# A recurrence of 32 heads: chunk by chunk over all heads, instead of four groups of heads inside the products

## The chip, the cores and the metric

The kernel runs on one core of a Trainium2 chip. The metric is the device time of one execution in microseconds, lower is better. Five engines matter: PE (TensorE, matrix products), ACT (ScalarE), DVE (VectorE), POOL (GpSimd) and SP (SyncE, which here issues every DMA). PEld stands for PE's weight loads, which overlap its matmuls.

## The reference, cut to what matters

The model has two layers; the change is in the first one's mixer (RWKV-7, 32 heads of 64, 272 tokens: 16 meta tokens and 256 others).

```python
r, k, v = xr @ w_rkv[0], xk @ w_rkv[1], xv @ w_rkv[2]
g = sigmoid(xg @ g1) @ g2
kk = normalized(k * k_k);  k = k * (1 + (a - 1) * k_a)
def step(S, inp):                       # per head, S is 64 x 64
    sa = einsum('bhvk,bhk->bhv', S, a_t)            # a_t = -kk
    S = S * w_t + sa[..., None] * b_t + v_t[..., None] * k_t    # b_t = kk * a
    return S, einsum('bhvk,bhk->bhv', S, r_t)
y = lax.scan(step, S0, ...)
y = group_norm(y) * ln_w + ln_b
bonus = sum(r * k * r_k, per head) * v
out = ((y + bonus) * g) @ w_o
```

Both layers have an MLP of width 8192 behind the mixer; the second mixer is gated linear attention. All of it is float32 in and out.

## The kernel before, in words

Activations lie transposed: 16 tiles (`KT`) of 128 features by `T` = 272 tokens. A large product splits each weight tile of 128x1024 into a high part (L134, ACT) and the rest (L135, DVE), and does three matmuls of 272 columns for each 128x128 block (`mm3`, L140 to L142).

The mixer works in this order. First come the r-products, the low-rank terms and gates' inner part. Then the **k-products** (L452 on): for each f of 16 feature tiles (two heads each) a product `proj`, a chain on ACT and DVE that makes the scaled keys and queries `bk` and `ar` (four `put`s, each a product over four chunks of 64 tokens and one over the last 16), their stores to DRAM (`bkd`, `ard`), a head sum `ss` (L465) and the bonus head sum `rk` (L480) on PE. Into these the first group's scores and its inversion are woven.

The recurrence is done in chunks: four of 64 tokens and a short one of 16. For a chunk, `scores` (L416) multiplies `BK` by `AR` for all token pairs, masked by DVE into `AM`; `invert` turns the triangular blocks of 32 rows into their inverses on DVE (30 steps of two operations, L268 `upd` and `sysA`, between transposes L431 to L449), and `merge` (L535, L545) joins two blocks of 32 to one of 64 on PE. Then follow, for a chunk: `centre` (values, L558), `inner` (L579), `state` (L598, L601), `solve` (L611), `carry` (L620) and `learn` (L626) for the new state, `emit` (L636) for the output, `keys` (L569) as transposes for learn. A chunk must wait for the state of the one before.

Heads go in **four groups of eight** (`NG` = 4), one group through its five chunks after the other. PE's order is written out by hand (`manual_schedule`): `R(n)` puts n steps of three product matmuls between the recurrence's batches, as the table `GAPS` says, 448 such steps in all: the v-products (`v_proj`, 16 x 16 steps), then the output products in pieces (`outA` over the first half of the heads, `outB` over the rest) as groups finish. While group g runs, group g + 1 gets its scores, inversion and merge; `norm` of group g - 1 makes the group norm and its gate product (L665).

PE, ACT, DVE and SP each take their instructions in order; PE's order is by hand here, the others' by a planner.

Of the kernel before, what the change touches and what calls it, by code (L numbers as in the profile page):

```python
# [23 lines left out]
TP = 288  # L24
# [19 lines left out]


GAPS = [[(4, 3), (4, 3), (8, 7), (8, 7), (6, 6)],
# [3 lines left out]

MARK = [134, 214, 286]


class Kern:
# [17 lines left out]
    def t(self, pool, shape, tag, bufs=1, dt=F32):  # L72
        return pool.tile(shape, dt, tag=tag, bufs=bufs, name=self.nm(tag))

# [49 lines left out]
    def wload(self, src, prio=2000):  # L124
        nc = self.nc
        with self.tc.high_priority(offset=prio) if prio else ExitStack():
            raw = self.t(self.wp, [P, 1024], "raw", self.raw_bufs)
            nc.sync.dma_start(raw, src)
            hi = self.t(self.wp, [P, 1024], "hi", self.hi_bufs, F32R)
            lo = self.t(self.wp, [P, 1024], "lo", self.hi_bufs, F32R)  # L130
            n = 1024 // self.split_parts
# [134 lines left out]
    def rwkv(self, done):  # L266
# [7 lines left out]
        bkd, ard = (self.t(self.dp, [KT, P, 576], n) for n in ("bkd", "ard"))  # L274
# [26 lines left out]
        rstd = self.rstd_from(ep, ss, T, 1.0 / D, NORM_EPS, "kn", 2)  # L301
# [35 lines left out]
        xr = [self.t(self.xp, [P, 2, T], "x", KT, F32R) for _ in range(KT)]  # L337
# [49 lines left out]
        st2 = [[self.t(ep, [P, 576], n, 2) for i in range(2)] for n in ("bk", "ar")]  # L387
        for x in st2[0] + st2[1]:
            nc.gpsimd.memset(x[:, 512:], 0.0)
        Wf = self.t(ep, [P, T + 1], "W")  # L390
        nc.gpsimd.memset(Wf[:, 0:1], 1.0)
        W = Wf[:, 1:]

        def put(dst, slot, a, b, skip=0):
            v = dst[:, :512].rearrange("q (c s t) -> q c s t", c=4, s=2)[:, :, slot]
            tt(v, a[:, : 4 * C].rearrange("q (c t) -> q c t", c=4), b[:, : 4 * C].rearrange("q (c t) -> q c t", c=4))
            o = 512 + 32 * slot
            tt(dst[:, o + skip : o + 16], a[:, 4 * C + skip :], b[:, 4 * C + skip :])

        def fetch(g, dst, src, a=0, b=576):  # L400
            nc.sync.dma_start(dst[g % 2][:, :, a:b], src[4 * g : 4 * g + 4, :, a:b].rearrange("f p n -> p f n"))

        def load(g):
            fetch(g, BKs, bkd)
            fetch(g, ARs, ard)

        def scores(g, c):
            BK, AR, AM, AMr = (b[g % 2] for b in (BKs, ARs, AMs, AMrs))
            n = C if c < NC4 else 32
            cs = slice(c * 128, c * 128 + 2 * n)  # L410

            pv = [self.ptr().rearrange("p (h m) -> p h m", h=4)[: 2 * n, :, : 2 * n] for _ in range(2)]
            for p in range(4):
                for q in range(2):
                    rows = slice(64 * q, 64 * q + 64)
                    nc.tensor.matmul(pv[q][:, p], BK[rows, p, cs], AR[rows, p, cs], start=True, stop=True)  # L416
            dst, mk = (AM[:, c], self.maskA) if c < NC4 else (AMr, self.maskR)
            for q in range(2):
                tt(dst[:, q::2], pv[q], mk.unsqueeze(1).to_broadcast([2 * n, 4, 2 * n]))

        def invert(g):
            AM, AMr = AMs[g % 2], AMrs[g % 2]
            X = sysA
            diag = lambda u: AM[64 + 32 * u : 96 + 32 * u, :, :, 32 * u : 32 * u + 32].rearrange("p c h t -> p t c h")
            part = [slice(8 * k, 8 * k + 8) for k in range(4)]
            nc.gpsimd.memset(X[64:96], 0.0)
            for u in range(2):
                for k in part:  # L430
                    nc.vector.transpose(X[32 * u : 32 * u + 32, k], diag(u)[:, k])  # L431
                    yield
            for k in part[:2]:
                nc.vector.transpose(X[96:128, k], AMr[32:64, :, k].rearrange("p h t -> p t h").unsqueeze(2)
                                    .to_broadcast([32, 8, 4, 8]))
                yield
            nc.gpsimd.memset(X.rearrange("p a b -> p (a b)")[:, ::33], 1.0)
            for s in range(1, 31):
                n, m = 31 - s, s
                w = self.t(lp, [P, 256], "upd", 1)[:, : n * m].rearrange("p (a b) -> p a b", a=n)  # L440
                tt(w, X[:, s + 1 :, s : s + 1].to_broadcast([P, n, m]), X[:, s : s + 1, :m].to_broadcast([P, n, m]))
                tt(X[:, s + 1 :, :m], X[:, s + 1 :, :m], w, ALU.add)
                yield
            for k in part:
                nc.vector.transpose(t11.rearrange("p c h s -> p s c h")[:, k], X[0:32].rearrange("p t s -> p s t")[:, k])
                yield
            for u in range(2):
                for k in part:
                    nc.vector.transpose(diag(u)[:, k], X[32 * u : 32 * u + 32, k])  # L449
                    yield  # L450

        for f in range(KT):  # L452
            r = rr[f]
            bk, ar = st2[0][f % 2], st2[1][f % 2]
# [3 lines left out]
            iW, kk, sq, kn = (self.t(ep, [P, T], n, 2) for n in ("iW", "kk", "sq", "kn"))  # L458
            nc.scalar.activation(W, ca[:, 0], AF.Exp, scale=-DECAY)
            nc.scalar.activation(iW, ca[:, 0], AF.Exp, scale=DECAY)  # L460
            nc.scalar.mul(kk, ps, self.vec("k_k", f))
            nc.scalar.activation(sq, kk, AF.Square)
# [6 lines left out]
            nc.vector.scalar_tensor_tensor(out=kk, in0=sq, scalar=1e12, in1=kk, op0=ALU.min, op1=ALU.mult)  # L469
# [6 lines left out]
            nc.vector.scalar_tensor_tensor(out=kn, in0=r, scalar=self.vec("r_k", f), in1=kn, op0=ALU.mult, op1=ALU.mult)  # L476
            put(ar, 1, r, W)
            nc.sync.dma_start(ard[f], ar)
# [3 lines left out]
            nc.vector.tensor_copy(WC[:, f], W[:, C - 1 : 4 * C : C])  # L482
            if f == 3:
                xv = mix(3, self.xp)
                early2.close()
                wl = ExitStack()
                lp = wl.enter_context(tc.tile_pool(name="wl", bufs=1, reuse_waits="tile"))
                BKs, ARs = ([self.t(lp, [P, 4, 576], n)] for n in ("BK0", "AR0"))
                AMs, AMrs = [self.t(lp, [P, NC4, 8, 128], "AM0")], [self.t(lp, [64, 8, 64], "AMr0")]
                sysA = self.t(lp, [P, 32, 32], "sysA")  # L490
                t11 = sysA.rearrange("p a b -> p (a b)")[64:96].rearrange("p (c h s) -> p c h s", c=NC4, h=8)
                nc.gpsimd.memset(sysA, 0.0)
            if f == 4:
                load(0)
            if f == 6:
                for c in range(5):
                    scores(0, c)
                inv = invert(0)
# [613 lines left out]
```

## Time and profile before

| | us |
|---|---|
| three runs: median (lowest to highest) | 2619.78 (2614.41 to 2630.18) |
| the profiled execution | 2614.87 |
| its span, first to last instruction | 2612.6 |
| PE, DVE, ACT busy | 2545.5, 1679.5, 1267.8 |
| mean granted clock of PE | 0.986 |

The profile shows one execution. Busy time of PE counts a matmul from its start to a modelled end; matmuls overlap, so a stretch with 100% busy can still hold less work than another. The granted clock is 1.0 or 0.5 at any moment; a stretch's number is the mean.

### The profile page before, as it was taken

Reading aid. Unit: us, or ns where it says so; the run is one execution under the profiler, and the core shown is the slowest. Engines: PE = TensorE matmul, PEld = TensorE weight load, DVE = VectorE, ACT = ScalarE, POOL = GpSimd, SP = SyncE. Lnnn points to the kernel's source line nnn. Section 1 sums busy time; section 2 is a strip of 40 time slices with the busy share of each in tenths; the row PEclk is TensorE's granted clock in tenths of the full one; section 3 lists DMA queues with packets and bytes.
Section 4 is the critical chain, followed back from the end, with each engine's and each line's share of the span. In section 5 each row is a group of like instructions: output and inputs, shape, how many; then the busy total and the mean of one; then the engine's idle time right before and its main releaser. Section 6 shows DMA issues by size and latency. Waiting matters only on the chain.

```text
span 2612.6 us, 47351 instructions
## 1 busy us (share of the span) xinstructions
PE 2545.5 (97%) x19308; PEld 2360.1 (90%) x19308; DVE 1679.5 (64%) x2802; ACT 1267.8 (49%) x2068; POOL 11.5 (0%) x32
## 2 busy tenths in 40 slices
PE   7998999989999999999999999999999999999998
PEld 7887988879999999999999999998888888888887
DVE  8677967764755545545546677777666656656665
ACT  5464645544544434434434455545555435445344
POOL 0000000000000000000000000000000000000000
PEclk9998999988999999999999999999999999999999
DMA  5566742323455555555555544454555555555554
GB/s 193 175 217 213 242 161 97 104 88 99 164 175 177 178 175 174 176 177 178 176 174 176 186 156 156 154 173 158 186 187 190 187 187 189 189 186 190 188 187 160
DMA packets 137193, 450.59 MB, mean 172 GB/s; under 512 B 15760, under 2 KB 23696, under 8 KB 136976
## 3 DMA queue, kind: packets, MB, share of 16 engines
q1 hardware_dynamic: 136976, 447.58, 51.0%
q8 instruction: 151, 2.47, 0.4%
q14 instruction: 66, 0.54, 0.1%
HBM read 431.53 MB, written 15.99 MB: 171 GB/s over the span
## 4 chain that ended last, share of the span: by engine, by line
PE 80%; DVE 3%; ACT 1%; issue 0%; DMA 0%; DVEq 0%; SPq 0%
PE pj L168 24%; PE pj L140 13%; PE pj L142 13%; PE pj L141 13%; PE pj L169 12%; DVE lo L135 1%; PE pt L665 0%; PE pu L950 0%; ACT hi L134 0%; PE pt L416 0%; PE pt L936 0%; DVE upd L268 0%; DVE sysA L431 0%; DVE sysA L268 0%; PE pu L601 0%
## 5 line engine op out<-in xcount | busy, mean ns | idle before, releaser
L134 ACT CAST hi<-raw 128x1024 fp32r<-128x1024 f32 (+1 forms) x834 | 813.5, 983 | 1065.9 <-PE pj L141 551.9
L135 DVE TENSOR_TENSOR lo<-raw,hi 128x1024 fp32r<-128x1024 f32 (+1 forms) x834 | 946.7, 1142 | 580.6 <-ACT hi L134 571.8
L140 PE MATMUL pj<-x,hi 128*128 128x272 f32 x2224 | 661.1, 297 | 7.4 <-ACT x L308 4.3
L142 PE MATMUL pj<-x,lo 128*128 128x272 f32 x2224 | 648.5, 292 | 0.1
L141 PE MATMUL pj<-x,hi 128*128 128x272 f32 x2224 | 646.4, 291 | 0.5 <-DVE x L268 0.5
L168 PE MATMUL pj<-x,hi 128*128 128x512 f32 x1664 | 586.1, 395 | 2.1 <-DVE cj L178 1.1
L169 PE MATMUL pj<-x,lo 128*128 128x256 f32 x1664 | 466.7, 281 | 0.8 <-DVE lo L135 0.8
L140 PEld LDWEIGHTS pj<-x,hi 128*128 128x128 f32 x2224 | 424.3, 191 | 15.2 <-ACT x L308 5.1
L141 PEld LDWEIGHTS pj<-x,hi 128*128 128x128 f32 x2224 | 426.9, 192 | 2.9 <-DVE x L268 0.7
L142 PEld LDWEIGHTS pj<-x,lo 128*128 128x128 f32 x2224 | 423.8, 191 | 1.9 <-DVE lo L135 0.7
L168 PEld LDWEIGHTS pj<-x,hi 128*128 128x128 f32 x1664 | 312.4, 188 | 76.1 <-issue 1.9
L168 PE MATMUL pj<-h,hi 128*128 128x512 f32 x1024 | 358.5, 394 | 0.0
L169 PEld LDWEIGHTS pj<-x,lo 128*128 128x128 f32 x1664 | 313.3, 188 | 1.7 <-DVE lo L135 1.1
L140 PE MATMUL pj<-h,hi 128*128 128x272 f32 x1024 | 294.7, 288 | 0.0
L142 PE MATMUL pj<-h,lo 128*128 128x272 f32 x1024 | 293.9, 287 | 0.0
L141 PE MATMUL pj<-h,hi 128*128 128x272 f32 x1024 | 293.6, 287 | 0.0
L169 PE MATMUL pj<-h,lo 128*128 128x256 f32 x1024 | 288.5, 282 | 0.0
L168 PEld LDWEIGHTS pj<-h,hi 128*128 128x128 f32 x1024 | 192.4, 188 | 44.5
L141 PEld LDWEIGHTS pj<-h,hi 128*128 128x128 f32 x1024 | 193.7, 189 | 0.0
L169 PEld LDWEIGHTS pj<-h,lo 128*128 128x128 f32 x1024 | 193.5, 189 | 0.0
L140 PEld LDWEIGHTS pj<-h,hi 128*128 128x128 f32 x1024 | 192.6, 188 | 0.0
L142 PEld LDWEIGHTS pj<-h,lo 128*128 128x128 f32 x1024 | 192.1, 188 | 0.0
(253 smaller groups left out, 2217.9 us busy)
## 6 DMA issues: line engine op xcount, KB each, us to landing
raw<-mlp_w_d SPq DMA_DIRECT2D x512, 512.0 KB, 3.3
raw<-gla_in_d SPq DMA_DIRECT2D x98, 512.0 KB, 3.3
raw<-w_rkv_d SPq DMA_DIRECT2D x80, 512.0 KB, 3.6
raw<-gla_o_d SPq DMA_DIRECT2D x32, 512.0 KB, 4.3
raw<-w_r_d SPq DMA_DIRECT2D x16, 512.0 KB, 3.3
raw<-rw_oA_d SPq DMA_DIRECT2D x16, 512.0 KB, 3.3
raw<-rw_oB_d SPq DMA_DIRECT2D x16, 512.0 KB, 3.3
ard<-ar SPq DMA_DIRECT2D x16, 288.0 KB, 3.6
```

Of the source, the lines that this page charges most:

```text
L134: nc.scalar.copy(hi[:, h], raw[:, h])
L135: nc.vector.tensor_tensor(out=lo[:, h], in0=raw[:, h], in1=hi[:, h].bitcast(F32), op=ALU.subtract)
L140: nc.tensor.matmul(out, hi[:, ws], xh, start=first, stop=False)
L141: nc.tensor.matmul(out, hi[:, ws], xl, start=False, stop=False)
L142: nc.tensor.matmul(out, lo[:, ws], xh, start=False, stop=last)
L168: nc.tensor.matmul(wide, hi[:, ws], x[kt][:, :, off : off + SEQ], start=kt == 0, stop=False)
L169: nc.tensor.matmul(ps[:, :SEQ], lo[:, ws], x[kt][:, 0, off : off + SEQ], start=False, stop=kt == nk - 1)
```

## The change: what it does

- **k-products.** All of `rk`, the scores and the inversion leave this stage. `bk` and `ar` become tiles of five chunks of 64 (the last padded with zeros), and the two products by `iW` become one of 640 elements. Stores go to `bkd` and `ard` laid out by chunk. Two small copies move from DVE to ACT.
- **v-products.** They hold all scores: 20 units of (chunk, eight heads), two per f for the first four f, then one; each unit has 16 matmuls of a 64x64 quarter instead of 8 of 64x128. `rk` is in each f. From f = 4 on, 0.34 inversion steps (`PACE`) go with each product step. An inversion now handles two chunks of all 32 heads on 128 rows; there are two, and a short one of 16 rows for the last chunk. The first inversion's merge is in here.
- **The recurrence** runs after the v-products with no product between: chunk by chunk, two halves (z = 0, 1) of 16 heads that alternate. `inner` of the next chunk is interleaved with `solve`; the state is updated by DVE in place of `carry` and four ACT operations; copies out of PSUM are shared between ACT and DVE. The second merge and all 16 gate products come behind chunk 1.
- **Norms and output products.** Seven output tiles are summed in seven banks while the 16 norms come in one after the other; the remaining nine follow as plain products.
- Operand tiles `x` of one pool become pairs (`xs`).

```diff
-GAPS = [[(4, 3), (4, 3), (8, 7), (8, 7), (6, 6)],
...
         for f in range(KT):
...
-            put(ar, 0, kk, Wf[:, :T], 1)
-            nc.vector.tensor_copy(ar[:, 0:513:128], kk[:, ::C])
-            tt(kk, kk, ca[:, 1])
-            put(bk, 1, kk, iW)
-            put(bk, 0, kn, iW)
-            nc.sync.dma_start(bkd[f], bk)
+            tt(ar[:, :, 0], five(kk), five(Wf))
+            nc.scalar.copy(ar[:, :, 0, 0], kk[:, ::C])
+            tt(kx[:, 1, :T], kk[:, :T], ca[:, 1])
+            tt(bk.rearrange("p c s t -> p s c t"), kx.rearrange("p s (c t) -> p s c t", c=5),
+               five(iW).unsqueeze(1).to_broadcast([P, 2, 5, C]))
+            nc.sync.dma_start(bkd[:, :, f].rearrange("c p n -> p c n"), bk.rearrange("p c s t -> p c (s t)"))
...
-            rk = self.pu()[:, :T]
-            nc.tensor.matmul(rk, self.bones, kn, start=True, stop=True)
-            nc.scalar.copy(r, rk)
...
-            if f > 7:
-                for _ in range(7):
-                    next(inv, None)
...
+        def uload(c, g):
+            t = slot("ring", 1024).rearrange("p (a f n) -> p a f n", a=2, f=4)
+            for i, d in enumerate((bkd, ard)):
+                nc.sync.dma_start(t[:, i], d[c][:, 4 * g : 4 * g + 4])
+            return t
+
+        def scores(t, c, g, bank):
...
+                    for u in range(2):
+                        nc.tensor.matmul(pv[q][n * u : n * u + n, p], t[rows, 0, p, C * u : C * u + n], ar,
+                                         start=True, stop=True)
...
+        def eliminate(X, n, rows):
+            for s in range(1, n - 1):
...
+                tt(w, x[:, s + 1 : n, s : s + 1].to_broadcast([k, a, m]), x[:, s : s + 1, :m].to_broadcast([k, a, m]))
+                tt(x[:, s + 1 : n, :m], x[:, s + 1 : n, :m], w, ALU.add)
+                yield
...
+        def merge1(i, banks):
+            for a in range(2):
+                am, t11, qs, pq = AMs[2 * i + a], (X, T2)[a], (TA, X)[a], banks[a]()
+                for h in range(32):
+                    o, k = 32 * (h % 4), 32 * (h // 4)
+                    nc.tensor.matmul(pq[o : o + 32, k : k + 32], am[64:96, h, 32:64], t11[64:96, h], start=True, stop=True)
+                for j in range(4):
+                    nc.scalar.copy(qs[96:128, j::4], pq[32 * j : 32 * j + 32, :256].rearrange("p (h t) -> p h t", h=8))
...
+        def sides(z, c):
+            full, n, nr, am, lo, up, at = geom(c)
+            ra, uv = ras[z, c], uvs[z, c]
+            nc.scalar.mul(uv[up, 0::2], ra[at[0]], -1.0)
+            nc.vector.tensor_scalar(out=uv[up, 1::2], in0=ra[at[1]], scalar1=-1.0, scalar2=None, op0=ALU.mult)
...
+        def solve(z, c):
...
+            for p in range(8):
+                for i in (2 * p, 2 * p + 1):
+                    o = n * (1 - i % 2)
+                    nc.tensor.matmul(pu[o : o + nu, p], am[up, 16 * z + i, :nu], uv[up, i], start=True, stop=True)
+                for i in (2 * p, 2 * p + 1) if both else ():
+                    inner1(z, c + 1, i)
+            nc.scalar.copy(uv[n : n + nu, 0::2], pu[n : n + nu])
+            nc.vector.tensor_copy(uv[n : n + nu, 1::2], pu[0:nu])
...
+        def gate(f):
+            g2 = self.t(kp, [P, 2, P], "g2", 2)
+            nc.sync.dma_start(g2, ap["g2"][f])
+            pg = self.ptr()[:, :T]
             for i in range(2):
+                nc.tensor.matmul(pg, g2[:, i], gs[i], start=i == 0, stop=i == 1)
+            nc.scalar.copy(gw(f), pg)
...
+        def norm(f):
+            sq = self.t(kp, [P, T], "ysq", 3)
+            nc.scalar.activation(sq, hres[:, f], AF.Square)
+            va = self.pm()[:, :T]
+            nc.tensor.matmul(va, self.bones, sq, start=True, stop=True)
...
         with tc.manual_schedule(engines={mybir.EngineType.PE}):
+            due = 0.0
+            for f in range(KT):
+                step = 0
+                for _ in v_proj(f):
+                    step += 1
+                    if f < 4 and step == 7 or step == 12:
+                        unit()
+                    if step == 13:
+                        rk = (self.pry if f % 2 else self.pm)()[:, :T]
+                        nc.tensor.matmul(rk, self.bones, rr[f], start=True, stop=True)
+                    if f >= 4 and merged[0] in (0, 3):
+                        due += PACE
+                        while due >= 1:
+                            due -= 1
+                            if next(inv, None) == "merge":
...
+            for c in range(5):
+                last = c == NC4
+                if c:
+                    state(0, c)
+                    learn(1, c - 1)
+                    emit(1, c - 1)
...
+                solve(0, c)
+                if c:
+                    state(1, c)
+                    if c < NC4:
+                        keys(1, c)
+                else:
+                    inner(1, 0)
+                    sides(1, 0)
+                some(inv, 4)
+                if not last:
+                    learn(0, c)
+                emit(0, c)
+                some(inv, 2)
+                solve(1, c)
+                if c < 3:
+                    bload(1, c + 1)
+                    keys(0, c + 1)
...
                 if c == 1:
                     some(inv, 99)
+                    merge1(1, (self.ptr, self.ptr))
+                    for f in range(8):
+                        gate(f)
+                    merge2(1, (self.ptr, self.ptr))
+                    for f in range(8, KT):
+                        gate(f)
...
+            norm(0)
+            norm(1)
+            NB = 7
+            pss = [b()[:, :T] for b in (self.pj, self.pj, self.ptr, self.ptr, self.pu, self.pu, self.pry)]
+            for kt in range(KT):
+                if kt + 2 < KT:
+                    norm(kt + 2)
+                ahead()
+                hi, lo = weights.pop(0)
+                for f in range(NB):
+                    self.mm3(pss[f], hi, lo, slice(f * P, f * P + P), yo[kt][:, 0], yo[kt][:, 1], kt == 0, kt == KT - 1)
```

More of the change, by code (lines that the diff above doesn't have):

```diff
@@ L400, in fetch @@
[L400 to L419, printed above, removed]
@@ L423, in invert @@
[L423 to L450, printed above, removed]
@@ new lines, in learn, with emit @@
+        def learn(z, c):
+            uv, pS = uvs[z, c], half(self.pu())
+            for i in range(16):
+                k = slice(64 * (i % 2), 64 * (i % 2) + 64)
+                nc.tensor.matmul(pS[k, i // 2], bkts[z][:, i // 2, k], uv[:, i], start=i < 2, stop=i > 13)
+            s, w = sb[:, 8 * z : 8 * z + 8], WC[:, 8 * z : 8 * z + 8, c].unsqueeze(2).to_broadcast([P, 8, HEAD])
+            if c:
+                tt(s, pS, s, ALU.add)
+            tt(s, s if c else pS, w)
+        def emit(z, c):
+            full, n, nr, am, lo, up, at = geom(c)
+            uv, ry = uvs[z, c], rys[z, c] if c else half((self.pry if z else self.pm)())
+            for i in range(16):
+                k = slice(64 * (i % 2), 64 * (i % 2) + 64)
+                nc.tensor.matmul(ry[k, i // 2, :nr], uv[: 2 * n, i], am[: 2 * n, 16 * z + i, n : n + nr],
+                                 start=c == 0 and i < 2, stop=i > 13)
+            nc.scalar.copy(hres[:, 8 * z : 8 * z + 8, c * C : c * C + nr], ry[:, :, :nr])
@@ L731, in rwkv @@
+        srcs = [s for f in range(KT) for s in pair(wv, f)] + [ap["rw_oK"][k] for k in range(KT)]
         weights = []
@@ L758, in some, with more, unit @@
                 next(it, None)
-        nothing = iter(())
+        order = [(c, g) for g in range(4) for c in range(2)] + [(c, g) for c in (2, 3) for g in range(4)]
+        order += [(4, g) for g in range(4)]
+        loaded = []
         self.split_parts = 2
-        load(1)
+        def more():
+            if order:
+                loaded.append((uload(*order[0]), *order.pop(0)))
+        def unit():
+            scores(*loaded.pop(0), self.pu if len(order) % 2 else self.ptr)
+            more()
@@ new lines, in rwkv @@
+            if merged[0] == 0:
+                while next(inv) != "merge":
+                    pass
+            bload(0, 0)
+            bload(1, 0)
+            centre(0, 0, ("x", "x"))
+            if merged[0] < 2:
+                merge1(0, (self.ptr, self.ptr))
+            keys(0, 0)
+            centre(1, 0, ("x", "x"))
+            if merged[0] < 3:
+                merge2(0, (self.ptr, self.ptr))
+            keys(1, 0)
+            inner(0, 0)
+            sides(0, 0)
+            aload(0, 1)
@@ L834, in rwkv @@
+        rec.close()
         self.split_parts = 1
+        for f in range(KT):
+            ps = pss[f] if f < NB else self.proj(pair(ap["rw_o"], f), yo, T)
+            tt(hres[:, f], ps, hres[:, f], ALU.add)
+            done(f)
         outer.close()
```

559 lines of the change are left out of this document (243 added, 316 removed), and 3 rows, old and new, of the table GAPS.

## The prediction

> **What bounds the kernel now.** I read the page's busy sums and slices first.
>
> ```profile
> PE 2545.5 (97%) x19308; PEld 2360.1 (90%) x19308; DVE 1679.5 (64%) x2802; ACT 1267.8 (49%) x2068; POOL 11.5 (0%) x32
> PEclk9998999988999999999999999999999999999999
> ```
>
> TensorE is busy for 97% of the span, so time can go only where its own work, its clock or its waits can. The page cannot show waits inside a "busy" stretch; the sums by stage can. Columns: stretch, length, then busy time (instructions) of PE, PEld, DVE, ACT and POOL, granted clock, DMA share, GB/s.
>
> ```profile
> 168.00:309.00 141.00, 131.69 (x920) 122.39 (x918) 124.68 (x334) 87.62 (x170) 2.06 (x3) 0.93 0.69 230
> 222.00:242.40 20.40, 16.78 (x96) 14.59 (x97) 12.18 (x32) 3.73 (x9) 0.00 (x0) 0.50 0.36 129
> 309.00:536.00 227.00, 214.20 (x2796) 191.22 (x2798) 169.81 (x399) 116.92 (x283) 4.88 (x9) 0.97 0.37 126
> 536.00:697.00 161.00, 151.50 (x1503) 139.04 (x1503) 97.20 (x206) 83.40 (x190) 0.99 (x3) 0.92 0.35 114
> 590.60:600.90 10.30, 10.30 (x210) 9.01 (x205) 2.79 (x6) 6.62 (x19) 0.52 (x1) 1.00 0.21 67
> 607.70:611.10 3.40, 3.40 (x40) 2.37 (x36) 0.00 (x0) 0.70 (x3) 0.00 (x0) 1.00 0.02 5
> 611.10:624.80 13.70, 13.70 (x83) 12.17 (x82) 3.43 (x6) 4.72 (x11) 0.00 (x0) 0.50 0.10 38
> 700.00:1463.00 763.00, 763.00 (x6115) 763.00 (x6114) 402.15 (x475) 326.49 (x414) 0.36 (x2) 1.00 0.53 176
> ```
>
> The change touches 168 to 697: the k-products (168 to 309), the values with the first groups (309 to 536), the rest of the recurrence with the output products (536 to 697), 141 + 227 + 161 = **529 us**. The last row prices an undisturbed product: 763 / 6115 = 0.125 us a matmul. Each of the three products has 16 x 16 x 3 = 768 matmuls, 96 us; 288 in all. So **241 us** of these 529 are small matmuls, waits and half clock (0.50 in the second and seventh rows, 34 us of it). Before 168 and after 697 nothing of weight changes.
>
> What a small job costs when it interrupts the products (start, length, what ran):
>
> ```profile
> 206.10 0.29 PE L140 MATMUL pt<-x,hi 128*128 128x272 f32 x1
> 206.22 0.72 PE L465 MATMUL pm<-sq,cst 128*128 128x272 f32 x2
> 206.57 0.49 PE L141 MATMUL pt<-x,hi 128*128 128x272 f32 x1
> 206.90 0.28 PE L142 MATMUL pt<-x,lo 128*128 128x272 f32 x1
> 207.02 0.29 PE L140 MATMUL pt<-x,hi 128*128 128x272 f32 x1
> ...
> 343.11 0.29 PE L142 MATMUL pj<-x,lo 128*128 128x272 f32 x1
> 343.32 1.16 PE L416 MATMUL pt<-AR,BK 64*128 64x128 f32 x16
> 344.41 0.39 PE L140 MATMUL pj<-x,hi 128*128 128x272 f32 x1
> 344.64 0.29 PE L141 MATMUL pj<-x,hi 128*128 128x272 f32 x1
> ```
>
> From 206.10 to 207.02 three product matmuls pass, 0.375, so one head sum (`ss`, and `rk` likewise) costs 0.92 - 0.375 = **0.55 us**. From 343.11 to 344.64 two pass, so one unit of scores costs 1.53 - 0.25 = **1.28**. Batches of the recurrence, for 8 heads:
>
> ```profile
> 349.16 0.69 PE L626 MATMUL pu<-uv,bkt 128*64 128x64 f32 x16
> 349.77 0.68 PE L579 MATMUL pu<-uv,AM 64*64 64x64 f32 x16
> 350.39 0.69 PE L636 MATMUL pry<-AM,uv 128*64 128x64 f32 x16
> 351.00 0.66 PE L569 MATMUL pm<-cst,BK 128*128 128x128 f32 x4
> 351.59 0.27 PE L601 MATMUL pu<-S,AR 64*64 64x64 f32 x1
> ...
> 352.21 0.38 PE L416 MATMUL pt<-AR,BK 64*128 64x128 f32 x2
> ```
>
> By their starts: learn, inner and emit 0.61 each, keys 0.59; the state's 16 matmuls (351.59 to 352.21) 0.62, though they are twice as many as inner's 8: four quadrants of the array ran at once, where inner has two.
>
> **k-products.** `rk`, the first group's scores and its inversion leave; the products by `iW` become one. Per f: 48 x 0.125 + 0.55 = 6.55; 16 of them 105, with 2 at the start **107**, against 141. What filled the difference: five score units at half clock (second row) and VectorE, 124.68 of 141 busy.
>
> ```profile
> L135 DVE TENSOR_TENSOR lo<-raw,hi 128x1024 fp32r<-128x1024 f32 (+1 forms) x834 | 946.7, 1142 | 580.6 <-ACT hi L134 571.8
> L268 DVE TENSOR_TENSOR upd<-sysA 128x30 f32<-128x30 f32 (+14 forms) x120 | 39.4, 328 | 2.6
> L268 DVE TENSOR_TENSOR AM<-pt,cst 128x512 f32<-128x512 f32 x32 | 20.7, 685 | 38.4 <-PE pt L416 38.4
> L268 DVE TENSOR_TENSOR ar<-r,W 128x256 f32<-128x256 f32 (+1 forms) x32 | 8.9, 292 | 0.1
> ```
>
> 30 inversion steps of two operations, 30 x 0.66 = 20 us, and 8 x 0.69 of masks leave. The joined product of 640 elements lies between 0.69 (the 512-element mask) and the 1.17 of the four it replaces (0.292 each); I take 0.8. VectorE keeps about 6.1 us per f, estimated as two casts of 1.14, this 0.8 and some 3 us of other products: under 6.55, so TensorE sets the pace; range 105 to 115.
>
> **Values with scores and inversions.** 96 + 20 units x 1.28 + 16 `rk` x 0.55 = 130. The quarters are twice the matmuls, four at a time, as the state's: same price; two at a time would add 20 x 1.1 = 22. VectorE from f = 4: casts 2.3, masks 1.37, one product 0.44, 16 x 0.34 = 5.4 steps of 0.66 = 3.6: 7.7 against TensorE's 6.0 + 1.28 + 0.55 = 7.8. That is a tie; I add 4 for queueing (0 to 10). Merges (TensorE's order of time, with the wait in brackets), the store and the gate's load (DMA issues: KB each, us to landing) and the gates (groups):
>
> ```profile
> 402.03 1.35 PE L535 MATMUL pt<-sysA,AM 32*32 32x32 f32 x64 [3.01 <-DVE sysA L445]
> 557.60 1.92 PE L535 MATMUL pt<-sysA,AM 32*32 32x32 f32 x64 [5.52 <-DVE sysA L445]
> ard<-ar SPq DMA_DIRECT2D x16, 288.0 KB, 3.6
> g<-g_d SPq DMA_DIRECT2D x16, 128.0 KB, 2.6
> L665 PE MATMUL pt<-gs,g 128*128 128x272 f32 x64 | 17.7, 397 | 0.0
> ```
>
> A merge's 32 matmuls of 32x32 took 1.35; now 64 in four strips instead of two: 1.35 to 2.7, I take 1.8, twice; with 1 for the copies between and a wait of 3 as in the first row: 8. The first unit of scores stands 2 us into the stage, behind the last f's vector chain (some 5), its store (3.6) and its own load (about 3): a wait of 7 with 2 more at half clock (0 to 13), because everything later is queued behind it on TensorE's fixed order. Sum 130 + 4 + 8 + 9 = **151**.
>
> **Bare chunks.** Without products between, a full chunk of two halves costs 2 x (state 1.24 + solve 1.24 + learn 1.22 + emit 1.22 + keys 1.2) = 12.2; inner costs nothing, since it runs in solve's free quadrants. ScalarE and VectorE empty each batch beside the other half's batches: between state and its solve stand learn and emit of the other half, 2.4 us, against a copy of about 0.7 (the 512-element mask's row) and a handshake. Chunks 0 to 4 I put at 12, 12.2, 12.2, 13, 9, the hand-over from the values at 8, centring and leftover waits 5.5: 72. Behind chunk 1 come merges with a wait as before, 6.6, and 16 gates. A gate is 17.7 / 16 = 1.1 us of TensorE, but its weights have two buffers and take 2.6 to land: (2.6 + 0.1 + 1.1) / 2 = 1.9 each, 30 us instead of 17.7 (which is the floor if loads hide). Sum **109**.
>
> **Output products.** 96 + 16 norm sums of 0.55 = 105; 4 at the start, where the first norm's seven operations hang after the last emit, and 3 where ScalarE and VectorE, each about 3 us per round of 2.62 + 0.55, get in the way: **112**. A few drops of the clock, 3.4 us each, cost 5 more.
>
> **Sum.** 107 + 151 + 109 + 112 + 5 = 484 against 529: 45 us less. The profiled execution took 2614.9, 4.9 below the median of the three runs, 2619.8; taken from the median it gives **2575 us**.
>
> **The rivals.**
>
> *Half clock in the bare chunks.* In 607.7 to 611.1 TensorE counts as busy throughout (3.40 of 3.40), and yet the next 13.7 us are granted 0.50: 64x64 and 32-wide batches with waits are not enough work. In 590.6 to 600.9, the same batches with more product matmuls among them held 1.00. At half clock a batch takes 0.97 instead of 0.57:
>
> ```profile
> 471.15 0.57 PE pu L611 x16
> ...
> 615.95 0.97 PE pu L611 x16
> ```
>
> That is 1.7 times; if it begins at the merge and lasts through chunks 2 to 4 (37 us) it costs 26, if from chunk 0 on (61 us) 43: 2601 to 2618. Against it: back-to-back batches use half the array or more. Chance 0.20. [...]
>
> *VectorE sets the pace.* If inversions fall behind, both merges wait 5.5 as in the second merge row (5 more in all), and each f from 4 on takes 9: + 1.2 x 12 = 15. Together 2595. Chance 0.12.
>
> *Better than summed.* The gates' loads hide (-12) and the first scores do not wait (-9): 2554. Chance 0.12.
>
> *Slower: hand-offs exposed.* If the halves do not cover each other, each of some 40 batches waits for its copy, about 1.2 us (48 us), the clock halves for all of it (43 more, of which some is hidden by these very waits; I take 30): 45 is turned into a loss of 33, **2653**. It decides when waits pass about 2.4 us, the cover counted above; the order of the batches speaks against it. Chance 0.08. [...] No run here shows the bare case.
>
> **How the numbers follow.** The forecast has 0.48. A measurement of this kernel tells about 0.5% from no change, 13 us: faster means under 2607. Forecast, VectorE, the better case and half of the first rival lie there: 0.48 + 0.12 + 0.12 + 0.10 = 0.82; the other half, 0.10, counts as the same, hand-offs as slower, 0.08. The range 2548 to 2611 leaves out the slower case and the tails of the first and third rival.
>
> **What would show it.** Right: k-products in about 107 us with no half clock; about 9 us per f for the first four values and 8 after; gate starts 1.9 us apart; about 12 us per chunk; clock 1.00 in the chunks. Wrong: TensorE waiting on VectorE's `upd` or `lo` through the values; clock 0.50 from the merge on; batches of one half starting only after copies of the same half.

## The result, and the profile after

The changed kernel took 2583.05 us (median of 4 runs, 2575.75 to 2590.95) beside 2617.97 for the kernel before (4 runs, 2614.41 to 2630.18): ratio 0.986, 95% interval 0.981 to 0.991. The forecast was 2575 us, with 2548 to 2611 as its range. The profiled execution took 2577.9 us with a span of 2575.4, against 2614.9 and 2612.6: 37 us less.

The page of the changed kernel, busy sums and granted clock:

```profile
PE 2496.7 (97%) x19604; PEld 2322.4 (90%) x19604; DVE 1627.9 (63%) x2536; ACT 1251.4 (49%) x1970; POOL 7.1 (0%) x31
...
PEclk9999998889999999999999999999999999999999
```

TensorE has 296 more instructions and 49 us less busy time; its share of the span is 97% as before. As before, the page cannot say where the 37 us went. The sums by stretch can (columns as in the prediction: stretch, length, busy time of PE, PEld, DVE, ACT and POOL with instructions, clock, DMA share, GB/s):

```profile
168.00:281.50 113.50, 109.43 (x816) 104.66 (x814) 97.64 (x178) 84.76 (x187) 0.28 (x2) 1.00 0.90 281
281.50:430.40 148.90, 132.57 (x1676) 122.32 (x1675) 107.56 (x229) 59.49 (x108) 0.31 (x2) 0.95 0.59 192
430.40:546.50 116.10, 96.62 (x2208) 80.64 (x2208) 50.10 (x109) 57.20 (x109) 2.00 (x3) 0.88 0.29 91
546.50:660.50 114.00, 111.90 (x826) 108.12 (x825) 86.43 (x159) 71.02 (x143) 0.48 (x2) 0.95 0.51 166
```

These are the k-products, the values with scores, the bare chunks and the output products: 113.5 + 148.9 + 116.1 + 114.0 = 492.5 us against 529 before, where the prediction had 484. The k-products give back 27.5 us. The other three together take 379 us where the kernel before needed 388, although they now hold the `rk` sums, the five score units and the inversion that the k-products lost.

For the experiments, the stages are measured between the same events in every trace: first to last head sum of the k-products (L414; L465 before), from there to the first `centre` matmul (L556), to the first norm sum (L667), to the first matmul that follows the mixer (L224). Starts are read from the timeline of each kernel:

| us | k-products | values | bare chunks | outputs | sum |
|---|---|---|---|---|---|
| before | 132.5 | | | | 522.7 |
| before, units spread | 133.9 | | | | 527.5 |
| before, first inversion out | 134.3 | | | | 523.8 |
| before, first units out | 118.0 | | | | 506.1 |
| after | 104.7 | 149.3 | 116.1 | 114.0 | 484.1 |
| units later | 104.6 | 146.4 | 112.4 | 113.7 | 477.0 |
| gates with five buffers | 104.0 | 150.7 | 105.8 | 113.4 | 473.9 |
| inner apart | 104.4 | 151.2 | 118.2 | 113.7 | 487.5 |
| scores whole | 103.5 | 149.7 | 113.3 | 113.9 | 480.4 |
| three `ca` | 100.2 | 150.8 | 114.4 | 114.9 | 480.3 |
| keep warm | 103.4 | 147.4 | 116.6 | 113.8 | 481.3 |
| stores in runs | 103.4 | 149.4 | 115.9 | 114.8 | 483.5 |
| two sizes | 100.3 | 149.3 | 107.7 | 114.8 | 472.1 |
| three together | 100.2 | 146.4 | 107.6 | 114.2 | 468.4 |

A stage that an edit does not touch varies between traces by 1.3 us in the k-products, 2 in the values, 3.7 in the bare chunks and 1.5 in the outputs. Smaller differences say nothing.

### The profile page after: what moved, and what is told of

It is laid out like the page before. It is cut to its first block, busy times and chain, and to the rows that moved or that the text cites. A ratio compares the mean times of both kernels' runs of the same rounds, so it can differ in the third digit from the quotient of the medians.

```text
span 2575.4 us, 47608 instructions
## 1 busy us (share of the span) xinstructions
PE 2496.7 (97%) x19604; PEld 2322.4 (90%) x19604; DVE 1627.9 (63%) x2536; ACT 1251.4 (49%) x1970; POOL 7.1 (0%) x31
## 4 chain that ended last, share of the span: by engine, by line
PE 91%; DVE 4%; DMA 3%; ACT 2%; issue 1%; SPq 0%; DVEq 0%; ACTq 0%
PE pj L167 24%; PE pj L139 14%; PE pj L141 14%; PE pj L140 14%; PE pj L168 12%; DMA ca<-cad 1%; PE pj L194 1%; DVE lo L134 1%; PE pt L140 1%; PE pt L139 1%; PE pt L141 1%; DVE upd L267 1%; DVE X L267 1%; PE pt L654 1%; DMA l<-lora_d 0%
## 5 line engine op out<-in xcount | busy, mean ns | idle before, releaser
L133 ACT CAST hi<-raw 128x1024 fp32r<-128x1024 f32 (+2 forms) x820 | 812.6, 997 | 1106.4 <-PE pj L140 582.4
L134 DVE TENSOR_TENSOR lo<-raw,hi 128x1024 fp32r<-128x1024 f32 (+2 forms) x820 | 945.9, 1158 | 595.8 <-ACT hi L133 587.8
L139 PE MATMUL pj<-x,hi 128*128 128x272 f32 x2144 | 631.0, 294 | 6.2 <-ACT x L307 4.1
L141 PE MATMUL pj<-x,lo 128*128 128x272 f32 x2144 | 621.8, 290 | 4.1 <-DVE lo L134 4.1
L140 PE MATMUL pj<-x,hi 128*128 128x272 f32 x2144 | 617.3, 288 | 0.0
L139 PEld LDWEIGHTS pj<-x,hi 128*128 128x128 f32 x2144 | 404.4, 189 | 13.9 <-ACT x L307 4.9
L141 PEld LDWEIGHTS pj<-x,lo 128*128 128x128 f32 x2144 | 403.9, 188 | 7.0 <-DVE lo L134 6.1
L140 PEld LDWEIGHTS pj<-x,hi 128*128 128x128 f32 x2144 | 407.3, 190 | 2.1 <-DVE x L267 0.2
L167 PEld LDWEIGHTS pj<-x,hi 128*128 128x128 f32 x1664 | 313.0, 188 | 76.4 <-issue 1.9
L168 PEld LDWEIGHTS pj<-x,lo 128*128 128x128 f32 x1664 | 314.1, 189 | 1.7 <-DVE lo L134 1.1
```

Of the source, the lines that this page charges most:

```text
L133: nc.scalar.copy(hi[:, h], raw[:, h])
L134: nc.vector.tensor_tensor(out=lo[:, h], in0=raw[:, h], in1=hi[:, h].bitcast(F32), op=ALU.subtract)
L139: nc.tensor.matmul(out, hi[:, ws], xh, start=first, stop=False)
L140: nc.tensor.matmul(out, hi[:, ws], xl, start=False, stop=False)
L141: nc.tensor.matmul(out, lo[:, ws], xh, start=False, stop=last)
L167: nc.tensor.matmul(wide, hi[:, ws], x[kt][:, :, off : off + SEQ], start=kt == 0, stop=False)
```

## The experiments

### What the k-products lost: three edits of the kernel before

**Units spread.** The first group's five score units stand two, two and one in f = 6, 7 and 8 instead of all in f = 6.

```diff
-            if f == 6:
-                for c in range(5):
+            if 6 <= f <= 8:
+                for c in range(2 * f - 12, min(2 * f - 10, 5)):
                     scores(0, c)
+            if f == 8:
                 inv = invert(0)
-            if f > 7:
-                for _ in range(7):
+            if f > 8:
+                for _ in range(8):
```

> The kernel before with the first group's five score units spread over f = 6, 7 and 8 (two, two, one) instead of all at f = 6, and its inversion steps from f = 9 at 8 per f instead of from f = 8 at 7. If the k-products lost their time in that cluster of units with its waits and its 20.4 us at half clock, the stage falls from 141 to about 118 to 124 us and the whole by 15 to 20, which would be more than half of what the change gained. Rival: VectorE, with products, casts and the inversion, sets that stage's pace: 135 us or more, the whole within 5 us of the kernel before.

2620.65 us, ratio 1.001 (0.999 to 1.004): nothing. The longest of TensorE's waits of this kernel between 204 and 290 us (line, waited for, us in total, times, longest) are no shorter than those of the kernel before in the same stretch, which were 2.5 for the masks, 2.5 for the same load, 1.9 for `sq` and 1.3 for `kn`:

```profile
PE pm L465 <- ACT sq L462: 3.1, 2, 1.9
PE pt L416 <- DMA AR<-ard: 3.1, 1, 3.1
PE pt L140 <- DVE AMr L268: 2.4, 1, 2.4
```

**First inversion out.** The 30 steps of the first group's inversion are left out; its inverse is then only the masked scores.

```diff
-            for s in range(1, 31):
+            for s in range(1, 31) if g else ():
```

> The kernel before without the 30 elimination steps of the first group's inversion (left out; its transposes stay). They are 60 operations of about 0.33 us, 20 us of VectorE, inside the k-products. If VectorE sets that stage's pace (58.09 of 59 us busy from 250 to 309), the stage falls from 141 to about 121 to 127 us and the whole by 14 to 20. Rival: the waits around the score units (wait for the first load of ard, 3 us, masks, half clock) set it: 135 us or more and less than 6 us of the whole.

2616.15 us, ratio 0.999 (0.998 to 1.000). The same 59 us of the k-products by stretches, first before, then without the inversion:

```profile
250.00:309.00 59.00, 57.16 (x411) 53.56 (x409) 58.09 (x167) 40.54 (x78) 0.00 (x0) 1.00 0.75 243
```

```profile
250.00:309.00 59.00, 57.43 (x404) 54.14 (x403) 50.96 (x136) 40.54 (x78) 0.00 (x0) 0.97 0.75 247
```

VectorE is busy 58.09 of 59 us before, which looks like the bound. With 7 us of its work taken away, no more matmuls pass in the same time (404 for 411). So an engine busy for 98% was not the pace here by itself. That TensorE, busy for 57.16 of the 59, was the other bound is read from the rows and not shown by a run. The clock blurs it a little: the trace of this kernel has 27.3 us at half clock in the k-products, that of the kernel before 20.5, so up to some 3 us of a gain may be hidden.

**First units out.** Here the scores themselves go (`AM` and `AMr` of the first group are zeros).

```diff
             if f == 6:
-                for c in range(5):
-                    scores(0, c)
+                nc.gpsimd.memset(AMs[0], 0.0)
+                nc.gpsimd.memset(AMrs[0], 0.0)
                 inv = invert(0)
```

> The kernel before, without the five score units of the first group and their masks (AM and AMr of that group are filled with zeros; the result is then not the reference's). Theory: these five units, the waits between them and the half clock that they start cost the k-products much more than their own TensorE work of 5 x 1.28 = 6.4 us: k-products from 141 to about 115 to 120 us, the whole 20 to 26 us faster than the kernel before, about 2594. Rival: only their own work and the masks go, the waits move to whatever follows (the inversion's operations, the next group's loads): 6 to 8 us, about 2611.

2601.45 us, ratio 0.9935 (0.992 to 0.995): 17 us, between the two. The k-products shrink by 14.5 (table), and the clock in them is whole:

```profile
168.00:293.70 125.70, 116.75 (x831) 108.95 (x831) 117.68 (x318) 85.41 (x166) 5.99 (x5) 1.00 0.79 258
```

So the five units cost 14.5 us where their own matmuls take 6.4: the other 8 us were waits and half clock around them (the row of 222.00 in the prediction has 20.4 us at 0.50). Spreading them does not remove it, taking them out of this stage does. Now VectorE begins to show: TensorE waits for its `kn` (L476) 4.8 us in this stage, 1.7 before. A kernel with units and inversion both left out was not run.

### The k-products of the changed kernel

The chain of waits of the changed kernel, a part of the k-products (start, us, what; the dots stand for pieces between), goes again and again through the landing of one tile:

```profile
181.52 5.05 DMA ca<-cad
...
191.02 6.01 DMA ca<-cad
...
205.57 5.17 DMA ca<-cad
```

`ca` holds the running sums that each f reads back from DRAM. It has two buffers, so a load starts only when f - 2 is done with its tile, and the DMA issues of the changed kernel, then of the kernel before (KB each, median us to landing), show that it takes longer to land than it did:

```profile
ca<-cad SPq DMA_DIRECT2D x16, 272.0 KB, 4.7
```

```profile
ca<-cad SPq DMA_DIRECT2D x16, 272.0 KB, 3.9
```

TensorE's own waits in this stage (168 to 282 us) are all at the head sum, whose operand is made behind that tile:

```profile
PE pm L414 <- ACT sq L410: 4.1, 7, 1.2
```

**Three `ca`.** `ca` gets a third buffer (so do two earlier users of that name, not shown); the space comes from one `W` buffer in place of two.

```diff
-        Wfs = [self.t(ep, [P, TQ + 1], "W", 2) for _ in range(2)]
+        Wfs = [self.t(ep, [P, TQ + 1], "W", 1)] * 2
...
-            ca = self.t(ep, [P, 2, T], "ca", 2)
+            ca = self.t(ep, [P, 2, T], "ca", 3)
```

> The changed kernel with three buffers instead of two for the loaded decay and gate rows (ca) and, to make room, one instead of two for W. The chain of the k-products goes through the landing of ca in six of 16 tiles, 4.4 to 6.0 us each. If the third buffer takes that landing off the chain, the stage (168 to 281.5, 113.5 us) falls to 106 to 109. Rival: TensorE's own work with the two casts on ScalarE and VectorE is the pace and the landing only fills: 112 us or more.

2575.46 us, ratio 0.984 (0.981 to 0.987). In the k-products of this kernel TensorE has no wait left, and head sum to head sum they are 4.5 us shorter:

```profile
168.00:275.50 107.50, 107.41 (x805) 103.94 (x803) 94.09 (x175) 80.48 (x184) 0.14 (x1) 1.00 0.94 291
```

**Stores in runs.** The change stores `bk` and `ar` by chunk, in pieces of 512 bytes; this kernel stores them by f, in rows of 2560 bytes, and lets the loads gather instead.

```diff
-            nc.sync.dma_start(bkd[:, :, f].rearrange("c p n -> p c n"), bk.rearrange("p c s t -> p c (s t)"))
+            nc.sync.dma_start(bkd[f].rearrange("p c n -> p (c n)"), bk.rearrange("p c s t -> p (c s t)"))
...
-                nc.sync.dma_start(t[:, i], d[c][:, 4 * g : 4 * g + 4])
+                nc.sync.dma_start(t[:, i], d[4 * g : 4 * g + 4, :, c].rearrange("f p n -> p f n"))
```

> The changed kernel with bkd and ard laid out by feature tile: a store writes rows of 2560 bytes instead of 512, and the later loads gather rows of 512. If the small packets (19188 of 512 bytes, 34.7 us of each DMA engine's time in the k-products, where the engines are 90% busy) slow the stage, it falls from 113.5 to 108 to 111 us, and loads in the stage of the values land some 0.5 us later, which two units of lead hide. Rival: the DMA engines are not the limit: 113 us or more, the whole unchanged within 3 us.

2581.56 us, ratio 0.987 (0.984 to 0.990). The k-products, whose DMA share falls from 0.90 to 0.85, are 1.3 us shorter, which is no more than the variation. `ca` lands in 4.3 us in place of 4.7 and TensorE's waits fall from 4.1 to 2.5 us, so the small packets may have a part in them; the third buffer removes all of them.

### The values

The chain where the values begin, and TensorE's own row (in brackets the idle time before it; `ring` is the tile that holds `bk` and `ar` for a unit of scores):

```profile
283.92 0.84 DVE bk L267
...
284.77 0.36 SPq L424
...
285.23 0.52 SPq L451
...
285.80 4.65 DMA ring<-ard
```

```profile
290.59 0.70 PE L462 MATMUL pt<-ring 64*64 64x128 f32 x8 [9.04 <-DMA ring<-ard]
```

The last f's vector chain, its store, the load of the same data and 9.04 us of waiting, where the prediction had 7, and 2 for half clock. The trace has that too: 0.50 from 284.0, within the wait, to 294.2.

**Units later.** The first scores stand one f later.

```diff
-        PACE = 0.34
+        PACE = 0.37
-                    if f < 4 and step == 7 or step == 12:
+                    if 1 <= f < 6 and step == 7 or f >= 1 and step == 12:
-                    if f >= 4 and merged[0] in (0, 3):
+                    if f >= 5 and merged[0] in (0, 3):
```

> The changed kernel with its 20 score units one value tile later: none beside f = 0, two beside f = 1 to 5, one from f = 6; inversion steps begin at f = 5 at a pace of 0.37 instead of 0.34. If the wait of 9.0 us ahead of the first unit (281.2 to 290.6) and the 10.2 us at half clock behind it are a pure loss, the stage of the values falls from 148.9 to about 138 to 140 us and the whole by about 9 to 11. Rival: the stage is paced by VectorE's inversions and the merge behind them, and the wait is only moved: 147 to 150 us, and no change of the whole beyond 3 us.

2582.11 us, ratio 0.985 (0.982 to 0.988). The values are 3 us shorter, not 9. The wait is smaller, not gone:

```profile
294.77 1.99 PE L462 MATMUL pt<-ring 64*64 64x128 f32 x32 [5.23 <-DMA ring<-ard]
```

The edit puts 16 more product steps, 6 us, ahead of the first scores, but the wait falls by only 3.8. The load is now issued late: on SyncE's queue it stands behind a weight load (L127) that goes out only at 288.81, though the store of the last `bk` was issued at 286.90 (timeline of this kernel):

```profile
288.81 0.34 SPq L127 DMA_DIRECT2D raw<-w_rkv_d  x1
289.25 0.38 SPq L451 DMA_DIRECT2D ring<-bkd  x1
```

**Scores whole.** In the four full chunks one 64x128 matmul takes the place of two 64x64 quarters.

```diff
+                    if c < NC4:
+                        nc.tensor.matmul(pv[q][:, p], t[rows, 0, p], t[rows, 1, p], start=True, stop=True)
-                    for u in range(2):
+                    for u in range(0 if c < NC4 else 2):
```

> The changed kernel with the scores of the four full chunks as one 64x128 matmul for each pair of heads and half instead of two 64x64 quarters: half as many matmuls in 32 of the 40 units, the same result. Prediction's view: quarters run four at a time, so a unit costs the same either way: 0 to +3 us over the changed kernel, 2583 to 2586. Rival: quarters cost more than whole blocks (two at a time): the whole blocks then save up to 1.1 us in each of 16 units that stand in the values' stretch: -10 to -18, about 2568.

2583.92 us, ratio 0.987 (0.985 to 0.989). The values take 149.7 with half as many matmuls in these units, 149.3 without. One unit in each timeline, whole and then in quarters:

```profile
344.84 1.16 PE L462 MATMUL pt<-ring 64*128 64x128 f32 x16
```

```profile
346.59 1.10 PE L462 MATMUL pt<-ring 64*64 64x128 f32 x32
```

Twice the matmuls in the same time: the quarters run four at a time, at the price of whole blocks.

### The bare chunks

The seven parts of this stage in the changed kernel: hand-over (both halves' first `centre`, `keys`, `inner`), chunk 0, chunk 1, the second merge with the gates, chunks 2, 3 and 4:

```profile
430.40:442.95 12.55, 7.76 (x80) 6.41 (x81) 11.61 (x34) 8.67 (x15) 0.12 (x1) 0.92 0.54 183
442.95:460.60 17.65, 15.50 (x264) 14.05 (x264) 8.31 (x26) 10.84 (x16) 0.00 (x0) 0.67 0.18 61
460.60:475.60 15.00, 12.31 (x401) 11.20 (x401) 4.81 (x7) 6.66 (x13) 0.94 (x1) 0.89 0.46 144
475.60:507.80 32.20, 24.14 (x324) 15.13 (x324) 7.52 (x15) 11.97 (x32) 0.00 (x0) 0.89 0.25 74
507.80:522.30 14.50, 14.10 (x433) 12.48 (x432) 6.00 (x9) 7.78 (x14) 0.94 (x1) 1.00 0.36 113
522.30:533.70 11.40, 11.40 (x393) 10.66 (x392) 5.98 (x9) 5.93 (x11) 0.00 (x0) 1.00 0.02 5
533.70:546.50 12.80, 11.42 (x324) 10.71 (x320) 5.87 (x9) 5.35 (x12) 0.00 (x0) 0.88 0.26 74
```

**Gates with five buffers.** The gates' weights move from two buffers of their own to the five of the norms' `ysq`, which is free then.

```diff
-            g2 = self.t(kp, [P, 2, P], "g2", 2)
+            g2 = self.t(kp, [P, T], "ysq", 5)[:, :256].rearrange("p (i n) -> p i n", i=2)
-            sq = self.t(kp, [P, T], "ysq", 3)
+            sq = self.t(kp, [P, T], "ysq", 5)
```

> The changed kernel with five buffers instead of two for the gates' weights (they share the norms' buffers, five instead of three). If the gates are limited by the landing of their weights (16 gates with two merges took 478.0 to 508.0, 30 us), they fall to about 1.2 us each and the stretch to 20 to 22 us; the whole by 8 to 10. Rival: the copies out of PSUM on ScalarE and the half clock (6.8 us of it there) set the pace: the stretch keeps 27 us or more, the whole within 3 us.

2575.96 us, ratio 0.982 (0.978 to 0.986). The last gates in the timeline, after and then with five buffers:

```profile
503.39 1.15 PE L654 MATMUL pt<-gs,g 128*128 128x272 f32 x4 [0.58 <-DMA g<-g_d]
505.01 1.15 PE L654 MATMUL pt<-gs,g 128*128 128x272 f32 x4 [0.47 <-ACT AM L655]
```

```profile
494.13 6.68 PE L654 MATMUL pt<-gs,ysq 128*128 128x272 f32 x28 [0.33 <-ACT AM L526]
```

Seven gates now run in one piece. First to last gate matmul takes 19.3 us in place of 29.4, and the bare chunks fall to 105.8: all of the 10 us arrives at the end of the stage.

**Inner apart.** `inner` of the next chunk runs behind `solve` instead of in its free quadrants.

```diff
-                for i in (2 * p, 2 * p + 1) if both else ():
-                    inner1(z, c + 1, i)
-            if c == 3:
+            if c < NC4:
                 for i in range(16):
-                    inner1(z, 4, i)
+                    inner1(z, c + 1, i)
```

> The changed kernel with the inner products of the next chunk behind solve instead of interleaved with it (chunks 0 to 2, both halves). If four quadrants of the array work at once only when interleaved, six batches of 16 matmuls at 1.22 us come back: the bare chunks take 7 us more (116.1 to about 123), the whole + 7. Rival: the batches run into waits anyway, or two quadrants at a time lose nothing: 0 to 2 us.

2585.39 us, ratio 0.987 (0.983 to 0.991). The pair of batches, after and then apart:

```profile
510.87:511.85 0.98, 0.98 (x68) 0.98 (x68) 0.83 (x2) 0.59 (x1) 0.00 (x0) 1.00 0.07 17
```

```profile
520.01:521.85 1.84, 1.84 (x68) 1.77 (x65) 0.60 (x1) 1.17 (x2) 0.00 (x0) 1.00 0.81 281
```

The pair's matmuls of 64x64 (68 instructions in each window, a few of them neighbours') need 0.98 us interleaved and 1.84 apart: the free quadrants are real. There are six such pairs, 6 x 0.86 = 5.2 us. The stage grew by 2, and its variation is 3.7: how much of the 5.2 is hidden by waits for copies can't be told from this run.

**Keep warm.** 18 matmuls that nothing reads stand at the first wait of the values and 6 at the hand-over, so that the array is not idle.

```diff
+        def warm(n):
+            pw = self.pry()
+            for _ in range(n):
+                nc.tensor.matmul(pw[:, :T], self.ones, self.vecs[:, :T], start=True, stop=True)
...
+                        if (f, step) == (0, 7):
+                            warm(18)
                         unit()
...
             sides(0, 0)
+            warm(6)
             aload(0, 1)
```

> The changed kernel with 24 matmuls that nobody reads put where TensorE waits anyway: 18 ahead of the first score unit, 6 ahead of the first solve. If the half clock of 10.2 us behind the first wait and of 13.7 us behind the hand-over comes from those waits and costs what the batches show (1.6 instead of 0.95 us for 16 heads), both stretches stay at 1.00 and the whole falls by 5 to 7. Rival: the clock falls for the thin batches and not for the wait, or the copies set the pace there: half clock stays in the first chunk and the whole changes by less than 2.

2575.24 us, ratio 0.985 (0.983 to 0.986). The hand-over and chunk 0 of this kernel:

```profile
428.40:440.92 12.52, 10.67 (x92) 8.60 (x92) 11.58 (x33) 8.65 (x15) 0.12 (x1) 1.00 0.52 179
440.92:459.40 18.48, 13.32 (x268) 11.98 (x268) 8.26 (x26) 10.78 (x16) 0.00 (x0) 0.82 0.18 59
```

The clock is 1.00 and 0.82 where it was 0.92 and 0.67, and the time is the same: 12.52 for 12.55 and 18.48 for 17.65. Faster batches only wait longer (2.1 us for L623, where the changed kernel has 0.7), and TensorE's waits of this kernel from 428.4 to 459 name the copies of VectorE and ScalarE:

```profile
PE pu L632 <- DVE x L623: 2.1, 1, 2.1
...
PE pu L632 <- ACT x L622: 1.4, 1, 1.4
PE pu L619 <- DVE x L573: 0.9, 1, 0.9
```

VectorE is full: 11.6 of the 12.5 us of the hand-over, in both kernels. The timeline of the changed kernel shows with what, and how it reaches TensorE. `inner` ends at 440.05, and from then on the two copies that `solve` needs (L572 on ACT, L573 on DVE) could run:

```profile
441.24 1.04 ACT L497 COPY AM<-TA 32x1024 f32<-32x1024 f32 x1 [1.64 <-DVE TA L494]
442.31 0.59 ACT L572 ACTIVATE x<-pj 64x512 f32<-64x512 f32 x1
442.95 0.47 PE L619 MATMUL pu<-x,AM 64*64 64x64 f32 x2 [2.90 <-ACT x L572]
443.20 0.20 DVE L267 TENSOR_TENSOR X<-X,upd 32x50 f32<-32x50 f32 x1
443.43 0.68 DVE L573 TENSOR_SCALAR x<-pj 64x512 f32<-64x512 f32 x1
```

ScalarE first waits for VectorE's last transpose (`TA`) of the second inversion and copies it (L497); only then comes the copy for `solve`, and TensorE has waited 2.90 us, its longest wait here. VectorE meanwhile runs steps on 32 rows (`X`, 32x50): those of the short inversion, from 441.24 to 448.22 with the copies of the chunk among them. The second inversion is due only behind chunk 1, the short one only for the last chunk. That they set the length of the hand-over and chunk 0 is read from these queues; a kernel with them moved was not tried.

### Edits together

**Two sizes** has the gates' five buffers and the three `ca`; **three together** has also the later units. Their diffs are those above.

> The changed kernel with the two buffer edits alone (five buffers for the gates' weights, three for the tile of k's products): 12 to 15 us less than the changed kernel if they add, about 2569; beside the kernel with three edits together it tells what the later start of the scores is worth: 3 us if it adds, nothing if the wait at the first scores is only moved.

> The changed kernel with three of the earlier edits together: the scores begin one f later, the gates' weights have five buffers, and the tile of one k and its neighbour has three buffers instead of two (and the W tile one). If the three act in different stretches and add: values 3 us less, gates 10 less, k-products 5 less, in all 15 to 18 less than the changed kernel, about 2566 (ratio 0.980). Rival: what one saves is waited for later by the next (the scores, one f later, press on the merges once the k-products end sooner): no more than the best of the three alone, about 2575.

Two sizes: 2561.12 us, ratio 0.978 (0.976 to 0.980). Three together: 2559.89 us, ratio 0.977 (0.975 to 0.979), the fastest version here, 60 us under the kernel before where the change has 35. Its stages are in the table.

By stages the three add: k-products 4.5 less, values 2.9, bare chunks 8.5, in all four stages 15.7 of the 15 to 18 expected; two sizes have 12.0 of 12 to 15. The medians differ by more, 23 us for the three; the two speeds of the last section, 10 us apart, can make such a difference. The rival, that one saving is waited for later, falls. The later units are worth 2.9 us in the values' stage; the two medians, 1.2 apart with overlapping intervals, cannot show it.

## Why the prediction was right, and where it was not

The forecast of 45 us less became 35 by the medians (24 to 49 by the interval), 37 in the profiled execution and 38.6 by the sum of the stages (522.7 to 484.1).

**k-products: 107 forecast, 113.5 measured.** The TensorE sum, 6.55 for each f, was right to 2%: the kernel with three `ca` takes 100.2 for 15 steps of f, 6.68 each, with TensorE full. The step that was missing is a wait on a load with two buffers once TensorE no longer hides it, 4.5 us from head sum to head sum and 6 by the rows from 168. The measured stage lies within the prediction's 105 to 115, but by luck: that range was meant for VectorE's work, which was 97.64 us, 6.1 for each f as forecast, and did not set the pace. And one reason for the old length was wrong: "VectorE, 124.68 of 141 busy", with its 20 us of inversion, cost nothing that shows by itself (first inversion out). What the stage gained, head sum to head sum, is 27.8 us: 14.5 for the units with their waits and half clock (measured), 16 x 0.55 = 8.8 for `rk` (worked out), 4.5 that no run separates. Of these, 6.4 and 8.8 were moved to the values.

**Values: 151 forecast, 148.9 measured.** Right in its terms: quarters four at a time (scores whole), the wait at the start (9.04 for 7) with half clock behind it, and the pace of the first f. Between head sums `rk` (L736) three steps of f with two units each took 26.84 us, 8.95 each for a forecast of 9. Later ones show VectorE; the rows are those three steps, then four from f = 5 on:

```profile
296.85:323.69 26.84, 26.84 (x345) 24.67 (x344) 16.26 (x28) 9.56 (x17) 0.00 (x0) 1.00 0.71 232
339.33:374.46 35.13, 31.90 (x330) 29.42 (x329) 34.00 (x77) 10.28 (x21) 0.00 (x0) 1.00 0.55 180
```

The four take 8.78 each where TensorE's sum is 7.8; VectorE is busy for 34.00 of 35.13 us. Most of TensorE's waiting from 300 to 430 us is for its `lo`, the sign that the prediction gave for the rival in which VectorE sets the pace:

```profile
PE pj L141 <- DVE lo L134: 3.9, 7, 1.0
```

So that rival came in part. It cost some 5 us over the five steps ahead of the first merge, about the 4 that the sum had for queueing, and not its 15: the last four steps of f, behind the first merge, took 7.2 to 7.8 again. Nor did the merges wait 5.5; the second, in the timeline, waited 0.40, and for ScalarE:

```profile
475.63 0.71 PE L515 MATMUL pt<-X,AM 32*32 32x32 f32 x62 [0.40 <-ACT lo L567]
```

**Bare chunks: 109 forecast, 116.1 measured.** Mis-sized were the hand-over (8, measured 12.5), the last chunk (9, measured 12.8) and chunk 0 (12, measured 17.65 with 4.7 of centring for the next chunks, for which, with leftover waits, the prediction had 5.5 in all the stage). What lengthens the hand-over, by the keep-warm run, is not the clock but the copies that come late there. The slower rival, in which each batch waits for its copy out of PSUM, shows mainly at the hand-over and in chunk 0, where TensorE waited up to 2.90 us for such copies, some 5 us instead of 48 in all (the last chunk has 1.4 more), and there the copies, 0.59 to 0.68 us each, were late behind the inversions' steps and not slow. Against it stood cheaper batches than assumed. In chunk 2 (timeline of the changed kernel) learn and emit for 16 heads start 0.98 apart, where the prediction took 1.22 from twice 8 heads:

```profile
508.86 1.15 PE L632 MATMUL pu<-x,lo 128*64 128x64 f32 x32
509.84 1.10 PE L643 MATMUL pry<-AM,x 128*64 128x64 f32 x32
```

Chunk 3, which has no centring, took 11.4 for a forecast of 13. The gates were right in size and cause: 36.6 forecast with the merge, 32.2 measured, 10 of it the two buffers.

**Outputs: 112 forecast, 114.0 measured**, right. The 5 us for drops of the clock were counted beside the stages; in the rows they are inside them.

**Half clock in the bare chunks** had 0.20. It came in part: 0.67 in chunk 0, 0.89 in the next two rows, 1.00 in chunks 2 and 3, and 0.88 in the last. Where it was deepest, less of it saved nothing (keep warm: 0.82 in chunk 0, and 18.48 us for 17.65). In the values' first wait (9.04 us idle) the clock fell 2.4 us into it, with the half clock from 284.0 to 294.2; at the hand-over it fell at 441.0, 1 us into a wait of 2.90, and stayed at half to 454.7. With the unread matmuls the values had 0.99 (281.0 to 428.4 of that kernel) where they had 0.95, and 441.0 to 454.7 had 0.75 for 0.50. How much idle time, or how little work, makes the clock fall no run shows; that small batches with waits are not enough work was the reading of one row (607.7 to 611.1 of the kernel before), an estimate of its author. In chunks 2 and 3, with TensorE busy for 25.5 of 25.9 us, such batches kept 1.00.

**What the other 9 us are.** Values, chunks and outputs fell from 388 to 379 while 15.2 us of work came in, 24 like for like. Worked out, not separated by a run: batches of 16 heads at 0.98 instead of 2 x 0.61, some 50 of them, 12 us; the `carry` step gone; inner in free quadrants, 2 to 5; fewer interruptions of the products. Against these stand the gates' loads (10) and the hand-over.

## What to carry to other kernels

When work leaves a stage, look at once for the load with two buffers that the work had hidden; the stage's TensorE sum was right to 2%, and the landing of one tile took 5 us of the gain. Before an engine at 98% is named as the pace, ask what is late when its work is gone: another may be nearly as full. And look for work that is due later, as the inversions here, ahead of copies that are due now on the same queue.

## What the runs showed of the hardware

The same instructions behind the changed part ran at two speeds. After the mixer the kernel has a long stretch of back-to-back products with clock 1.00 and TensorE busy throughout; in two profiled executions (after, then gates with five buffers) it holds

```profile
700.00:1420.00 720.00, 720.00 (x5770) 720.00 (x5770) 378.30 (x446) 306.54 (x385) 0.36 (x2) 1.00 0.52 176
```

```profile
700.00:1420.00 720.00, 720.00 (x5686) 720.00 (x5685) 373.32 (x439) 301.71 (x379) 0.36 (x2) 1.00 0.52 174
```

5770 or 5686 matmuls in 720 us, 1.5% apart, with nothing else in the rows to tell them apart. From L224 to the end the slower ones took 1924.5 to 1924.9 us, the others 1913.2 to 1915.2: 10 us. Five of ten profiled executions of the changed kernel and its variants had the lower speed, none of the four of the kernel before and its variants; but one of the four runs of the kernel before, which was not profiled, took 2630.18 us beside 2614 to 2620, so the change need not be its cause. The 10 us can be part of the spread of a kernel's runs (15 us for the changed kernel) and of what medians of four of its variants differ by beyond their edits, which no run separates; for them the stages above are compared up to L224 alone. Their cause stays open.

The changed kernel had the half clock, between 168 and 660 us, for 10.2 us from 284.0, for 13.7 from 441.0 and 543.4 each, and for 3.4 from 393.2, 468.3, 478.6 and 495.6 each. Six unread matmuls at the hand-over raised it there from 0.92 to 1.00 and in chunk 0 from 0.67 to 0.82; that this was worth nothing (12.52 us for 12.55, 18.48 for 17.65) was the surprise.
